# Expert blocks of at most 64 tokens with high and low parts side by side in one stationary operand

## The chip, the cores and the metric

The kernel runs on one core of a Trainium2 chip. The metric is the device time of one execution in microseconds. Before the change it is 1669.88 us, the median of three runs (1667.90 to 1670.72).

## What is computed

One layer over 1024 tokens of width 1024: a state-space branch and a short convolution, merged and projected, and then a mixture of 32 experts in four groups. Only the experts matter here. Each token goes to two experts of one group, and each expert computes on its tokens

```python
hid = jax.nn.silu(xblk @ w_gate[e]) * (xblk @ w_up[e])
return hid @ w_down[e]
```

with `w_gate` and `w_up` 1024 x 512 and `w_down` 512 x 1024, all in float32. The routing of the given inputs sends very different numbers of tokens to the experts. In the order in which the kernel works through them (`seq`) they are 194, 46, 56, 6, 140, 20, 55, 27, 77, 31, 47, 22, 106, 56, 48, 11, 143, 22, 8, 5, 117, 47, 32, 69, 62, 169, 106, 11, 193, 79, 12, 31. So 21 of the 32 have at most 64 tokens, 6 have 65 to 128, and 5 have more than 128; of these five second blocks three have at most 64 tokens (12, 15, 41), and two have 66 and 65.

## The kernel before, in words

The first half of the kernel (to about 885 us) computes the mixers and the routing. The rest is a Python loop over the 32 experts (from L1822, written out in full in the program). The order of the instructions on every engine is the order in which the code is written; no scheduler moves them.

Precision: a float32 operand is split into a high part `hi` (a ScalarE copy to fp32r, L91) and a low part `lo` (VectorE, source minus high part, L92). A product is then three matmuls (`mm3`, L94): high by high, high by low, low by high.

One expert's weights arrive as six tiles of 1 MB (`raw`, 128 x 2048), issued on SP's queue (`dma_w`, L1519) each time an older one has been split. `spl(e, i)` (L1655) splits tile `i` in two halves: two ScalarE copies of 128 x 1024 and two VectorE subtractions. That makes 12 ScalarE and 12 VectorE instructions for an expert.

A block of up to 128 tokens is gathered to `xg` (128 x 1024, one token a partition; partitions without a token keep zeros or old rows). `xhalf` (L1670) transposes half of it on TensorE into PSUM (`tp`) and splits it to `xh` and `xl`. `part(e, q, o)` (L1679) multiplies half `q` with the gate (`o` = 0) or up (`o` = 1) weights: four slices of three matmuls with 512 columns. The two halves add up in one PSUM bank for gate and one for up (`GU`). `act` (L1683) takes SiLU of the gate bank on ScalarE and multiplies it with the up bank on VectorE. `hsplit` (L1688) transposes the result on TensorE and splits it to `hh` and `hl`. `down` (L1696) is 24 matmuls into `ybank`; `emit` weights the rows and scatters them to DRAM from GpSimd.

The body of the loop interleaves expert e with expert e + 1: the second half of gate and up of e, then `spl(e + 1, 1)`, `act`, `spl(e, 4)`, the first half of gate of e + 1, `hsplit`, `spl(e, 5)`, the first half of up of e + 1, `down`, and three more splits. Three run-time conditions (`tc.If`) stand in it, for second blocks of experts with more than 128 tokens: L1831, L1844 and L1851 (which holds L1852 and L1858). Every engine executes the branch of every `If`, also one that has nothing in its body. The block count of an expert is read from SBUF into a register (`get_nb`, L1758).

Of the kernel before, what the change touches and what calls it, by code (L numbers as in the profile page):

```python
# [33 lines left out]
SLOTS = 128  # L34
NB = 8
# [14 lines left out]
def block_kernel(ctx: ExitStack, tc: tile.TileContext, I, out):  # L50
# [1201 lines left out]
    def pick(pl, i):  # L1252
        rr = sb(pl, "rr", [P, 2, 6, NE], BF16, bufs=3)
# [5 lines left out]
    def place(pl, i, b0, rr, ps):  # L1259
        oa = sb(pl, "oa", [P, 2, 2 * P], BF16, bufs=3)  # L1260
# [377 lines left out]
    by_seq = nbi.rearrange("p (g m) -> p m g", g=4)  # L1638
# [31 lines left out]
    def xhalf(xg, q, nm="x"):  # L1670
# [17 lines left out]

    def hsplit(hf, a="hh", b="hl"):
        a, b = sb(wk, a, [P, 4, P], F32R), sb(wk, b, [P, 4, P], F32R)  # L1690
# [27 lines left out]
    def over(e, q, banks):  # L1718
        if q == 0:
            warm(banks[0], 1.3)  # L1720
        xs = xhalf(xos[e % 2], q, "o")
        for o in range(2):
            part(e, q, o, xs, banks[o])

    full = xgs[0][:, 0:NB * NE * 3].rearrange("p (b e f) -> p b e f", b=NB, e=NE)

    def more(e, wf, banks, banks2):
# [21 lines left out]
        ht = tr(act(banks, "so"), "xf", 0)  # L1749
# [8 lines left out]
    def get_nb(e):  # L1758
        if e not in NBV:
            NBV[e] = load_nb(e)  # L1760
        return NBV[e]

    def load_pair(e):
        return nc.values_load(nbp[0:1, e:e + 1], min_val=0, max_val=NB)
# [3 lines left out]

    GU = [[sb(psm, f"{x}{i}", [P, FF]) for x in "gu"] for i in range(2)]
    ybank = [sb(psm, f"y{n}", [P, 512]) for n in range(2)]  # L1770
    warm(ybank[0], 4.7)
    XA = xhalf(xgs[0], 0)
    take_lo((2, 3), V)
    XB = xhalf(xgs[0], 1)
# [3 lines left out]
    for o in range(2):  # L1778
        part(0, 0, o, XA, GU[0][o])
    for x in xos:  # L1780
        G.memset(x, 0.0)
    take_lo((4, 5), V)
    for e in range(2):
        nb = get_nb(e)
        with tc.If(nb > 1):
# [6 lines left out]
    nb = get_nb(0)  # L1792
    with tc.If(nb > 1):
# [29 lines left out]
    for e in range(NE):  # L1823
# [3 lines left out]
        if nxt:  # L1827
            XA = xhalf(xgs[(e + 1) % NX], 0)
        part(e, 1, 1, XB, A[1])
        spl(e + 1, 1)  # L1830
        with tc.If(get_nb(e) > 1):  # L1831
            over(e, 1, B)
            sgo = act(B, "so")
# [3 lines left out]
        sg = act(A)  # L1837
        if nxt:
            spl(e, 4)
        if nxt:  # L1840
            part(e + 1, 0, 0, XA, B[0])
        hs = hsplit(sg)
        if e + 2 < NE:
            with tc.If(get_nb(e + 2) > 1):  # L1844
                gather(xos[e % 2], e + 2, 1)
        if nxt:
            spl(e, 5)
            XB = xhalf(xgs[(e + 1) % NX], 1)
            gather(xgs[(e + 1) % NX], e + 1 + NX, 0)
            part(e + 1, 0, 1, XA, B[1])  # L1850
        with tc.If((load_pair(e) if nxt else get_nb(e)) > 1):  # L1851
            with tc.If(get_nb(e) > 1):  # L1852
# [164 lines left out]
```

## Time and profile before

| | |
|---|---|
| median of three runs | 1669.88 us |
| the profiled execution | 1674.46 us, span 1672.6 us |
| TensorE matmul busy | 1570.5 us (94%) |
| VectorE busy | 1320.1 us (79%) |
| ScalarE busy | 725.3 us (43%) |
| GpSimd busy | 330.5 us (20%) |
| mean granted TensorE clock | 0.984 |
| DMA over the span | 381.61 MB, mean 228 GB/s |

The busy shares are means over stages that differ. The expert loop takes from about 885 us to 1610 us, so a change in it is read from a window inside it. An engine's row names the line of the code; the word after a window's busy times is the granted clock, then the share of the DMA engines' time.

### The profile page before, as it was taken

Reading aid. Unit: us, or ns where it says so; the run is one execution under the profiler, and the core shown is the slowest. Engines: PE = TensorE matmul, PEld = TensorE weight load, DVE = VectorE, ACT = ScalarE, POOL = GpSimd, SP = SyncE. Lnnn points to the kernel's source line nnn. Section 1 sums busy time; section 2 is a strip of 40 time slices with the busy share of each in tenths; the row PEclk is TensorE's granted clock in tenths of the full one; section 3 lists DMA queues with packets and bytes.
Section 4 is the critical chain, followed back from the end, with each engine's and each line's share of the span. In section 5 each row is a group of like instructions: output and inputs, shape, how many; then the busy total and the mean of one; then the engine's idle time right before and its main releaser. Section 6 shows DMA issues by size and latency. Waiting matters only on the chain.

```text
span 1672.6 us, 23420 instructions
## 1 busy us (share of the span) xinstructions
PE 1570.5 (94%) x7602; PEld 1237.4 (74%) x7602; DVE 1320.1 (79%) x2917; ACT 725.3 (43%) x1053; POOL 330.5 (20%) x264
## 2 busy tenths in 40 slices
PE   7899999899998899999988999999999999999984
PEld 3688888778886777788866777777777777777751
DVE  7858883569998568878876786999986999686877
ACT  1533332341213342231122664777764777465622
POOL 1431000002234300003213121221221212120127
PEclk9999999999998999999989999999999999999998
DMA  8425788742314665656524695999995999676872
GB/s 320 163 76 167 230 244 263 239 166 98 100 60 131 167 179 164 202 194 229 184 77 162 251 340 191 348 364 363 362 345 182 361 356 377 259 284 240 290 296 101
DMA packets 141731, 381.61 MB, mean 228 GB/s; under 512 B 17632, under 2 KB 76160, under 8 KB 116992
## 3 DMA queue, kind: packets, MB, share of 16 engines
q1 hardware_dynamic: 130912, 362.80, 62.2%
q0 software_dynamic: 10656, 16.80, 2.7%
q8 instruction: 83, 1.36, 0.3%
q14 instruction: 80, 0.66, 0.1%
HBM read 336.98 MB, written 68.76 MB: 243 GB/s over the span
## 4 chain that ended last, share of the span: by engine, by line
PE 34%; DMA 24%; issue 21%; DVE 17%; POOL 1%; SPq 1%; POOLq 1%; another core or an unknown queue 0%; ACT 0%; DVEq 0%; ACTq 0%
DMA y_d<-yt,tbi 13%; DMA xo<-h_d,tbi 8%; DVE vs L911 4%; DVE sa L908 4%; PE g L95 3%; PE g L97 3%; PE g L96 3%; PE t L97 2%; PE t L95 2%; PE t L96 2%; PE pm L95 1%; DVE vc L911 1%; PE pm L96 1%; PE pm L97 1%; DVE acc L784 1%
## 5 line engine op out<-in xcount | busy, mean ns | idle before, releaser
L92 DVE TENSOR_TENSOR lo<-raw,hi 128x1024 fp32r<-128x1024 f32 x376 | 440.9, 1221 | 31.5 <-ACT hi L91 21.4
L91 ACT ACTIVATE hi<-raw 128x1024 fp32r<-128x1024 f32 x376 | 372.0, 1051 | 34.0 <-PEq L1858 20.8
L95 PE MATMUL g<-hh,wh 128*128 128x512 f32 x448 | 177.1, 395 | 0.0
L96 PE MATMUL g<-hl,wh 128*128 128x512 f32 x448 | 174.7, 390 | 0.0
L97 PE MATMUL g<-hh,wl 128*128 128x512 f32 x448 | 174.6, 390 | 0.0
L1715 POOL DMA_INDIRECT y_d<-yt,tbi x37 | 92.3, 2495 | 382.0 <-DVE yt L1708 300.4
L95 PE MATMUL y<-hi,hh 128*128 128x512 f32 x256 | 103.0, 402 | 6.1 <-PEq L1858 2.1
L92 POOL TENSOR_TENSOR wl<-raw,wh 128x1024 fp32r<-128x1024 f32 x17 | 41.1, 2419 | 330.8 <-ACT wh L91 330.8
L95 PE MATMUL g<-hi,xh 128*128 128x512 f32 x256 | 102.5, 400 | 4.2 <-ACT xh L91 0.3
L95 PE MATMUL u<-hi,xh 128*128 128x512 f32 x256 | 105.8, 413 | 0.0
L97 PE MATMUL g<-hi,xl 128*128 128x512 f32 x256 | 100.6, 393 | 1.1 <-DVE xl L92 1.1
L97 PE MATMUL u<-hi,xl 128*128 128x512 f32 x256 | 100.9, 394 | 0.0
L97 PE MATMUL y<-hi,hl 128*128 128x512 f32 x256 | 100.5, 392 | 0.0
L96 PE MATMUL g<-lo,xh 128*128 128x512 f32 x256 | 100.3, 392 | 0.0
L96 PE MATMUL u<-lo,xh 128*128 128x512 f32 x256 | 99.9, 390 | 0.0
L96 PE MATMUL y<-lo,hh 128*128 128x512 f32 x256 | 99.8, 390 | 0.0
L91 ACT ACTIVATE xh<-tp 128x512 fp32r<-128x512 f32 x64 | 37.5, 588 | 140.7 <-PE tp L1675 140.7
L95 PEld LDWEIGHTS g<-hh,wh 128*128 128x128 f32 x448 | 84.3, 188 | 19.1 <-issue 2.3
L97 PEld LDWEIGHTS g<-hh,wl 128*128 128x128 f32 x448 | 84.2, 188 | 17.9
L96 PEld LDWEIGHTS g<-hl,wh 128*128 128x128 f32 x448 | 84.3, 188 | 16.7
L610 ACT ACTIVATE sg<-g 128x512 f32<-128x512 f32 x32 | 19.2, 599 | 140.1 <-PE g L97 104.8
L1551 POOL DMA_INDIRECT xg<-h_d,tbi x32 | 34.0, 1063 | 213.6 <-PE tp L1675 160.1
(503 smaller groups left out, 3581.6 us busy)
## 6 DMA issues: line engine op xcount, KB each, us to landing
raw<-in_w_exp SPq DMA_DIRECT2D x192, 1024.0 KB
raw<-in_w_r SPq DMA_DIRECT2D x28, 512.0 KB
w<-w_d SPq DMA_DIRECT2D x32, 384.0 KB
raw<-in_w_ada SPq DMA_DIRECT2D x20, 512.0 KB
sig_d<-sg SPq DMA_DIRECT2D x32, 256.0 KB
rp<-r_d SPq DMA_DIRECT2D x64, 128.0 KB
raw<-in_w_ada SPq DMA_DIRECT2D x6, 1024.0 KB
aw<-in_w_ada SPq DMA_DIRECT2D x12, 512.0 KB
```

What stands on the lines that cost most here:

```text
L91: S.activation(hi, src, AF.Copy)
L92: (eng or V).tensor_tensor(lo, src, hi.bitcast(F32), op=ALU.subtract)
L95: PE.matmul(ps, a[0], b[0], start=first, stop=False)
L96: PE.matmul(ps, a[0], b[1], start=False, stop=False)
L97: PE.matmul(ps, a[1], b[0], start=False, stop=last)
L610: S.activation(sg, pg, AF.Sigmoid)
L784: V.scalar_tensor_tensor(acc, w[:, k, :], sc[:, k, 0:1], acc, op0=ALU.mult, op1=ALU.add)
L908: V.tensor_tensor(t[d], cur[:, d].unsqueeze(2).to_broadcast([P, 2, 2, NPAIR]), kc[:, d], op=ALU.mult)
L911: V.tensor_tensor(new[:, d], new[:, d], t[d][:, r], op=ALU.add)
L1551: G.indirect_dma_start(out=xg, out_offset=None, in_=h2_d, in_offset=bass.IndirectOffsetOnAxis(ap=tbi[:, b, seq[e], 0:1], axis=0), bounds_c ...
L1715: G.indirect_dma_start(out=y_d, out_offset=bass.IndirectOffsetOnAxis(ap=tbi[:, b, seq[e], 1:2], axis=0), in_=yt, in_offset=None, bounds_ch ...
```

## The change

For a block of at most 64 tokens (`HB`), the high parts of the 64 token columns and their low parts stand side by side in one 128-column stationary operand `xh`. One matmul with the high weights and one with the low weights then give rows 0 to 63 (high part of the tokens) and rows 64 to 127 (low part), and the two halves of the rows are added later. The third matmul of each slice is left out for such blocks; for the others it follows in `part_low`. The addition happens in the step that transposes: `both` is two 64 x 64 identities on top of each other, and a matmul of 128 rows of the gate bank with it transposes and adds at once (`fold`). For that both banks are copied to SBUF first (`sg`, `us`), and SiLU and the product come behind the transposition, on 128 x 256. Which way a block goes is decided at run time: counts are now in units of 64 (`nbh`), and `xhalf`, `part_low`, `act` and `hsplit` each hold a `tc.If`.

```diff
+    nbh = iotab[:, 0:2 * NE].bitcast(I32)
+    V.tensor_scalar(nbh, pc, HB - 1.0, None, op0=ALU.add)
+    V.tensor_scalar(nbh, nbh, 6, None, op0=ALU.logical_shift_right)
...
+    both = sb(xgp, "both", [P, HB])
+    V.tensor_add(both, ident[:, 0:HB], ident[:, HB:P])
+
-    def xhalf(xg, q, nm="x"):
+    def xhalf(xg, q, nb, lim, nm="x"):
...
-        split(xh, xl, pt)
+        S.activation(xh, pt, AF.Copy)
+        with tc.If(nb < lim) as few:
+            V.tensor_tensor(xh[:, :, HB:P], pt[:, :, 0:HB], xh[:, :, 0:HB].bitcast(F32), op=ALU.subtract)
+        with few.Else():
+            V.tensor_tensor(xl, pt, xh.bitcast(F32), op=ALU.subtract)
         return xh, xl
 
     def part(e, q, o, xs, ps_):
         for z in range(4):
-            mm3(ps_, (xs[0][:, z, :], xs[1][:, z, :]), piece(e, 2 * q + o, z, FF), q == 0 and z == 0, q == 1 and z == 3)
-
-    def act(pgu, nm="sg"):
+            w = piece(e, 2 * q + o, z, FF)
+            PE.matmul(ps_, xs[0][:, z, :], w[0], start=(q == 0 and z == 0), stop=False)
+            if q == 0 or z < 3:
+                PE.matmul(ps_, xs[0][:, z, :], w[1], start=False, stop=False)
+
+    def part_low(e, q, xs, banks, nb, lim):
+        with tc.If(nb >= lim):
+            for o in range(2):
+                for z in range(4):
+                    PE.matmul(banks[o], xs[1][:, z, :], piece(e, 2 * q + o, z, FF)[0], start=False, stop=False)
+        if q:
+            for o in range(2):
+                PE.matmul(banks[o], xs[0][:, 3, :], piece(e, 2 + o, 3, FF)[1], start=False, stop=True)
...
+    def fold(sg, us, pt):
+        ps_ = flat(pt).rearrange("p (x k t) -> p x k t", x=2, k=4)
+        for x, src in enumerate((sg, us)):
+            for k in range(4):
+                PE.matmul(ps_[:, x, k], src[:, k * P:(k + 1) * P], both, start=True, stop=True)
+        S.activation(halves(sg), ps_[:, 0], AF.Silu)
+        V.tensor_mul(halves(sg), halves(sg), ps_[:, 1])
+
+    def act(banks, us, nb, lim, nm="sg", now=False):
         sg = sb(wk, nm, [P, FF])
-        S.activation(sg, pgu[0], AF.Silu)
-        V.tensor_mul(sg, sg, pgu[1])
+        with tc.If(nb < lim) as few:
+            S.activation(sg, banks[0], AF.Copy)
+            S.activation(us, banks[1], AF.Copy)
+            if now:
+                fold(sg, us, sb(psm, "tp", [P, 4, P], bufs=2))
+        with few.Else():
+            S.activation(sg, banks[0], AF.Silu)
+            V.tensor_mul(sg, sg, banks[1])
         return sg
...
+    def hsplit(sg, us, nb, lim, a, b):
         pt = sb(psm, "tp", [P, 4, P], bufs=2)
-        for k in range(4):
-            PE.transpose(pt[:, k, :], hf[:, k * P:(k + 1) * P], ident)
-        split(a, b, pt)
+        with tc.If(nb < lim) as few:
+            if us is not None:
+                fold(sg, us, pt)
+            split(a[:, :, 0:HB], b[:, :, 0:HB], halves(sg))
+        with few.Else():
+            for k in range(4):
+                PE.transpose(pt[:, k, :], sg[:, k * P:(k + 1) * P], ident)
+            split(a, b, pt)
         return a, b
...
         part(e, 1, 0, XB, A[0])
         if nxt:
-            XA = xhalf(xgs[(e + 1) % NX], 0)
+            XA = xhalf(xgs[(e + 1) % NX], 0, get_nb(e + 1), 2)
         part(e, 1, 1, XB, A[1])
+        part_low(e, 1, XB, A, get_nb(e), 2)
+        us = sb(wk, "us", [P, FF])
         spl(e + 1, 1)
-        with tc.If(get_nb(e) > 1):
+        with tc.If(get_nb(e) > 2):
...
-        sg = act(A)
+        sg = act(A, us, get_nb(e), 2)
...
-        hs = hsplit(sg)
+        hs = hsplit(sg, us, get_nb(e), 2, *HS)
...
             part(e + 1, 0, 1, XA, B[1])
+            part_low(e + 1, 0, XA, B, get_nb(e + 1), 2)
```

How this moves the instructions is seen in the built programs. First ScalarE, in the body of one expert from the second block's `If` to the next pair of weight splits; `sg` is SiLU's result, `hi` the high part of a weight half, `hh` that of the hidden rows, `tp` the PSUM tile of a transposition. Before:

```order
L1831 COMPARE_AND_BRANCH
L91 ACTIVATE oh_11728<-tp 128x512
L1685 ACTIVATE so<-g_9272 128x512
L1831 UNCONDITIONAL_BRANCH x2
L1685 ACTIVATE sg<-g_9274 128x512
L91 ACTIVATE hi<-raw 128x1024 x2
L91 ACTIVATE hh<-tp 128x512
L1767 TENSOR_LOAD nbi
L1844 COMPARE_AND_BRANCH
L1844 UNCONDITIONAL_BRANCH x2
L91 ACTIVATE hi<-raw 128x1024 x2
```

The same stretch with the change, from behind the second block's `If` (the rows between a COMPARE_AND_BRANCH and the first UNCONDITIONAL_BRANCH are the way of at most 64 tokens, those up to the second one the other way):

```order
L1723 ACT_TABLE_LOAD
L1723 ACTIVATE sg<-g_9280 128x512
L1724 ACTIVATE us<-u_9281 128x512
L1722 UNCONDITIONAL_BRANCH
L1728 ACT_TABLE_LOAD
L1728 ACTIVATE sg<-g_9280 128x512
L1722 UNCONDITIONAL_BRANCH
L92 ACT_TABLE_LOAD
L92 ACTIVATE hi<-raw 128x1024 x2
L1738 COMPARE_AND_BRANCH
L1717 ACT_TABLE_LOAD
L1717 ACTIVATE sg<-tp 128x256
```

and, a few rows later, behind the condition on the gather of a second block (L1902) and ahead of the splits of tile 5:

```order
L1825 TENSOR_LOAD iotab
L1902 COMPARE_AND_BRANCH
L1902 UNCONDITIONAL_BRANCH x2
L92 ACT_TABLE_LOAD
L92 ACTIVATE hi<-raw 128x1024 x2
```

Between the same weight splits stand activation-table loads that were not there: four on the way of at most 64 tokens (L1723, L92, L1717, L92) and three on the other (L1728, L92, L92), in every expert of the loop. In the whole program there are 7 such rows before and 295 now.

Second TensorE, from the first half of gate of expert e + 1 to the first half of its up product, before:

```order
L97 MATMUL g_9272<-hi,xl_9777 128x512
L1693 MATMUL tp<-ident,sg 128x128 x4
L1767 TENSOR_LOAD nbi
L1844 COMPARE_AND_BRANCH
L1844 UNCONDITIONAL_BRANCH x2
L1675 MATMUL tp<-ident,xg_9271 128x128 x4
L95 MATMUL u_9273<-hi,xh_9776 128x512
```

and with the change:

```order
L1695 MATMUL g_9280<-lo,xh_9833 128x512
L1738 COMPARE_AND_BRANCH
L1716 MATMUL tp<-both,sg 128x64 x4
L1716 MATMUL tp<-both,us 128x64 x4
L1738 UNCONDITIONAL_BRANCH
L1744 MATMUL tp<-ident,sg 128x128 x4
L1738 UNCONDITIONAL_BRANCH
L1825 TENSOR_LOAD iotab
L1902 COMPARE_AND_BRANCH
L1902 UNCONDITIONAL_BRANCH x2
L1682 MATMUL tp<-ident,xg_9273 128x128 x4
L1684 COMPARE_AND_BRANCH
```

The four transpositions stand in one arm of a condition, eight folding matmuls in the other, and a further condition follows the transpositions of the next block; in an expert's body each engine passes six conditions more than before (L1684 twice, L1698 twice, L1722, L1738).

## Rows read from the trace of the kernel before

**Rows 1.** The page: busy time, share of the span and count of each engine.

```profile
PE 1570.5 (94%) x7602; PEld 1237.4 (74%) x7602; DVE 1320.1 (79%) x2917; ACT 725.3 (43%) x1053; POOL 330.5 (20%) x264
```

**Rows 2.** Windows, two experts without a second block; the first line names the columns.

```profile
core 0: us, PE busy (x) PEld busy (x) DVE busy (x) ACT busy (x) POOL busy (x), PEclk, DMA share, GB/s
1100.10:1118.74 18.64, 18.34 (x86) 14.59 (x85) 17.70 (x19) 13.86 (x16) 3.89 (x3) 1.00 0.99 370
1156.03:1174.66 18.63, 18.33 (x86) 14.57 (x85) 17.71 (x19) 13.86 (x16) 3.89 (x3) 1.00 0.98 361
```

**Rows 3.** Waits, 1081.45 to 1193.30 us (six experts): us in total, times, longest.

```profile
ACT xh L91 <- PE tp L1675: 19.5, 6, 3.3
ACT hh L91 <- PE tp L1693: 7.5, 6, 1.3
PEld y L95 <- ACTq L1851: 3.3, 6, 0.6
```

**Rows 4.** Groups of instructions, the same six experts, ScalarE and VectorE.

```profile
L91 ACT ACTIVATE hi<-raw 128x1024 fp32r<-128x1024 f32 x72 | 70.9, 1050 | 0.9 <-ACTq L1851 0.7
L91 ACT ACTIVATE hh<-tp 128x512 fp32r<-128x512 f32 x6 | 3.6, 599 | 7.5 <-PE tp L1693 7.5
L92 DVE TENSOR_TENSOR xl<-tp,xh 128x512 fp32r<-128x512 f32 x12 | 8.2, 684 | 0.0
```

**Rows 5.** Timeline, TensorE in the same expert: start us, us, instruction.

```profile
1103.63 0.40 PE L97 MATMUL u<-hi,xl 128*128 128x512 f32 x1
1104.18 0.47 PE L95 MATMUL g<-hi,xh 128*128 128x512 f32 x1
...
1107.02 0.60 PE L1693 MATMUL tp<-ident,sg 128*128 128x128 f32 x4
1107.46 0.60 PE L1675 MATMUL tp<-ident,xg 128*128 128x128 f32 x4
...
1111.75 0.39 PE L95 MATMUL y<-hi,hh 128*128 128x512 f32 x1
...
1116.33 0.39 PE L97 MATMUL y<-hi,hl 128*128 128x512 f32 x1
```

**Rows 6.** Timeline, ScalarE in the first expert (in its second block, and behind it).

```profile
918.13 1.28 ACT L1685 ACT_TABLE_LOAD   x1
921.51 0.60 ACT L1685 ACTIVATE so<-g 128x512 f32<-128x512 f32 x1 [2.09 <-PE g L97]
922.12 1.28 ACT L1685 ACT_TABLE_LOAD   x1
923.42 0.60 ACT L1685 ACTIVATE sg<-g 128x512 f32<-128x512 f32 x1
```

**Rows 7.** Groups by form: the nearest instructions of 128 x 256 that read PSUM.

```profile
L882 ACT ACTIVATE vj<-t 128x256 f32<-128x256 f32 x32 | 12.3, 385 | 6.1 <-PE t L97 5.0
L92 DVE TENSOR_TENSOR ul<-t,uh 128x256 fp32r<-128x256 f32 x16 | 6.7, 422 | 10.1 <-ACT uh L91 10.1
```

**Rows 8.** Timeline, ScalarE in an expert without a second block.

```profile
1101.79 2.00 ACT L91 ACTIVATE hi<-raw 128x1024 fp32r<-128x1024 f32 x2
1103.91 0.60 ACT L1685 ACTIVATE sg<-g 128x512 f32<-128x512 f32 x1
1104.40 2.00 ACT L91 ACTIVATE hi<-raw 128x1024 fp32r<-128x1024 f32 x2
```

**Rows 9.** Windows, the first expert's second block (columns as in rows 2).

```profile
899.70:902.20 2.50, 0.00 (x0) 0.01 (x1) 0.70 (x1) 0.00 (x0) 1.59 (x1) 1.00 0.87 323
904.30:907.40 3.10, 3.10 (x8) 2.44 (x8) 2.36 (x2) 1.07 (x2) 0.00 (x0) 0.50 0.91 374
```

**Rows 10.** One tensor's instructions (the index table `tbi`): gathers of second blocks.

```profile
L1551 POOL DMA_INDIRECT xo<-h_d,tbi x5: 999/1750/1777, 892.8 to 1486.6; - x5
```

**Rows 11.** Timeline, VectorE ahead of the expert loop.

```profile
887.62 0.18 DVE L1635 TENSOR_SCALAR nbi<-misc 128x32 int32<-128x32 f32 x1
887.84 1.74 DVE L1636 TENSOR_SCALAR nbi<-nbi 128x32 int32<-128x32 int32 x1
```

More of the change, by code (lines that the diff above doesn't have):

```diff
@@ L34 @@
 SLOTS = 128
+HB = 64
 NB = 8
@@ new lines, in flat, with halves @@
+    def flat(t_):
+        return t_.rearrange("p a b -> p (a b)")
+    def halves(sg):
+        return sg[:, 0:4 * HB].rearrange("p (k t) -> p k t", k=4)
+    def fold(sg, us, pt):
[5 more added lines that the diff above has]
+        V.tensor_mul(halves(sg), halves(sg), ps_[:, 1])
@@ new lines, in act @@
+    def act(banks, us, nb, lim, nm="sg", now=False):
+        sg = sb(wk, nm, [P, FF])
+        with tc.If(nb < lim) as few:
[6 more added lines that the diff above has]
+            V.tensor_mul(sg, sg, banks[1])
+        return sg
+    HS = [sb(wk, x, [P, 4, P], F32R) for x in ("hh", "hl")]
@@ L1691, in hsplit @@
+    for t_ in HS:
+        G.memset(t_.bitcast(F32), 0.0)
+    def hsplit(sg, us, nb, lim, a, b):
         pt = sb(psm, "tp", [P, 4, P], bufs=2)
-        for k in range(4):
-            PE.transpose(pt[:, k, :], hf[:, k * P:(k + 1) * P], ident)
-        split(a, b, pt)
+        with tc.If(nb < lim) as few:
[6 more added lines that the diff above has]
+            split(a, b, pt)
@@ L1748, in more @@
                               start=(q == 0 and z == 0), stop=(q == 1 and z == 3))
-        ht = tr(act(banks, "so"), "xf", 0)
+        so = sb(wk, "so", [P, FF])
+        S.activation(so, banks[0], AF.Silu)
+        V.tensor_mul(so, so, banks[1])
+        ht = tr(so, "xf", 0)
         for k in range(4):
@@ L1779, in block_kernel @@
         part(0, 0, o, XA, GU[0][o])
+    part_low(0, 0, XA, GU[0], get_nb(0), 2)
     for x in xos:
@@ L1791, in block_kernel @@
     scatter(zt, NE - 1, 0)
-    nb = get_nb(0)
-    with tc.If(nb > 1):
+    with tc.If(get_nb(0) > 2):
         over(0, 0, GU[1])
@@ L1827, in block_kernel @@
         if nxt:
-            XA = xhalf(xgs[(e + 1) % NX], 0)
+            XA = xhalf(xgs[(e + 1) % NX], 0, get_nb(e + 1), 2)
         part(e, 1, 1, XB, A[1])
+        part_low(e, 1, XB, A, get_nb(e), 2)
+        us = sb(wk, "us", [P, FF])
         spl(e + 1, 1)
-        with tc.If(get_nb(e) > 1):
+        with tc.If(get_nb(e) > 2):
             over(e, 1, B)
-            sgo = act(B, "so")
+            sgo = act(B, us, get_nb(e), 4, "so", True)
         if not nxt:
@@ L1847, in block_kernel @@
             spl(e, 5)
-            XB = xhalf(xgs[(e + 1) % NX], 1)
+            XB = xhalf(xgs[(e + 1) % NX], 1, get_nb(e + 1), 2)
             gather(xgs[(e + 1) % NX], e + 1 + NX, 0)
             part(e + 1, 0, 1, XA, B[1])
-        with tc.If((load_pair(e) if nxt else get_nb(e)) > 1):
-            with tc.If(get_nb(e) > 1):
-                h_ = hsplit(sgo, "oh0", "ol0")
+            part_low(e + 1, 0, XA, B, get_nb(e + 1), 2)
+        with tc.If((load_pair(e) if nxt else get_nb(e)) > 2):
+            with tc.If(get_nb(e) > 2):
+                h_ = [sb(wk, x, [P, 4, P], F32R) for x in ("oh0", "ol0")]
+                for t_ in h_:
+                    G.memset(t_.bitcast(F32), 0.0)
+                hsplit(sgo, None, get_nb(e), 4, *h_)
                 banks = [sb(psm, "tp", [P, 512], bufs=2) for _ in range(2)]
@@ L1857, in block_kernel @@
             if nxt:
-                with tc.If(get_nb(e + 1) > 1):
+                with tc.If(get_nb(e + 1) > 2):
                     over(e + 1, 0, A)
```

26 lines of the change are left out of this document (12 added, 14 removed).

## Prediction

> **What bounds the kernel now.** The page's busy shares come first [rows 1]: TensorE 94%, ScalarE only 43%. They are means over the whole kernel, so the reader should go to windows of the expert loop. An expert without a second block takes 18.64 us, again and again [rows 2], and there TensorE is busy for 18.34 of it, VectorE for 17.70, ScalarE for 13.86, at a granted clock of 1.00 (the upper level, 2.4 GHz), and the DMA engines for 0.98 to 0.99 of their time. The waits say which of the four ends last: ScalarE waits for TensorE's transpositions (19.5 + 7.5 us in six experts), TensorE for no engine's data, only at branches (0.55 us at L1851) [rows 3]. So TensorE sets the pace. VectorE is 0.9 us behind it, the DMA engines 0.2 to 0.4 us, and ScalarE has 18.64 - 13.86 = 4.78 us of room in an expert. These three rooms are what the change has to live with.
>
> A matmul's record lasts 0.39 us, but 20 of them start within 1116.33 - 1111.75 = 4.58 us [rows 5]: one costs 0.229 us. The 72 of an expert are 16.5 us; the rest of the 18.64 is transpositions and gaps at branches.
>
> **What it takes away.** For a block of at most 64 tokens, 16 of the 48 gate and up matmuls go: 16 x 0.229 = 3.7 us of TensorE. VectorE works on half the columns four times (two `xl`, the product, `hl`): 0.68 becomes 0.42 [rows 4, 7], about 1.0 us. It applies to 21 of 32 experts (token counts above).
>
> **What it adds on ScalarE** decides. On the way of at most 64 tokens, each term in us an expert:
> - four activation-table loads at 1.28 [rows 6]: +5.13. They are nearly pure time: the load at 922.12 ends at 923.40, the next instruction starts at 923.42. The table that it loaded was the one that the condition's arm had loaded 4 us earlier for the same function, so a load that changes nothing cost the same;
> - two copies of a bank in place of one SiLU, at 0.60 each [rows 8]: +0.60;
> - SiLU over 128 x 256, 0.385 [rows 7]: +0.39;
> - `hh` over 256 columns, 0.60 to the same 0.39 [rows 4, 7]: -0.21.
>
> 13.86 + 5.91 = 19.77 us of ScalarE work, over 18.64 before anything waits. To it come a lost overlap (ScalarE instructions overlap by 0.1: the one at 1103.91 lasts 0.60, the next starts at 1104.40 [rows 8]; table loads don't), 0.1; the wait of `hh` for VectorE's product, which now stands between SiLU and `hh` with nothing in between: 0.42 [rows 7] and some 0.1 for the two handovers, 0.5; and six more conditions. The two splits at 1101.79 end at 1103.79 and SiLU starts at 1103.91 [rows 8], so L1831 cost ScalarE 0.12 us; I take 0.1 for each, 0.6 (bounds 0 and 1.9, by TensorE's 0.32 a condition below). Together 21.0 us: **ScalarE becomes the bound**, 2.36 us over the old period.
>
> TensorE in such an expert needs about 18.64 - 3.7 + 0.5 + 1.0 = 16.4 us: four transpositions and a condition take 0.44 us [rows 5], eight folding matmuls on half the columns in their place at most about 0.9, and the conditions some 1.0. It is idle some 4 us in 21. After 2.5 us of idleness at 899.70 its granted clock was 0.50 (the lower level, 1.2 GHz) from 904.30 to 907.40 [rows 9], 8 matmuls in 3.1 us, where 1.83 would do at the upper level. The longest idle stretch lies between the second half of `up` and the first half of gate of the next expert, which waits for VectorE's `xh`; at half the clock those eight matmuls take 1.3 us longer, and ScalarE's third load waits for the fold behind them. Nothing in ScalarE's order hides more than about 1 us there. Bounds 0 and 1.1; I take 0.4.
>
> So 2.8 us for an expert. The last of the 21 has no next expert beside it, and its 3.7 us from TensorE stand against two loads, copy and fold in a row: nothing. 20 x 2.8 = **56 us**.
>
> **The 6 experts of 65 to 128 tokens** keep all 72 matmuls. ScalarE gets three loads: 13.86 + 3.85 + 0.6 = 18.3, still below TensorE. TensorE has the six conditions; from 1103.63 to 1104.18 the step is 0.55 instead of 0.229 [rows 5], so L1831 cost 0.32 us there. Some are empty on TensorE and lie between matmuls already queued: 0.2 each, 1.2 us. And the transpositions of `sg` come sooner after the last gate and up matmul: eight matmuls stand between, 1.83 us, not twelve, while SiLU has a load ahead of it: 1.28 + 0.60 + 0.68 + 0.3 = 2.9 us; less 1.83 and a branch leaves 0.8. Together 2.0 us (bounds 0.8 and 3.5): 6 x 2.0 = **12 us**.
>
> **The 5 experts with a second block** (five gathers `xo` [rows 10]): 2.0 as above, six more conditions in the second block at 0.2, 1.2; in three of them 3.7 us of matmuls go, against 1.2 for two copies that TensorE now waits for and 0.9 for the fold, mean -0.9 over the five. With 0.1 for a load on their longer chains, 2.4 (bounds 0.5 and 5): **12 us**.
>
> **Start and tail.** Ahead of the loop VectorE gets two more integer operations on 32 columns, like the rows of 0.18 and 1.74 us [rows 11], and the first transposition's split now waits for the count: 2 us (bounds 0.5 and 4). The rest of the program is the same; the smaller pools of `pick` and `place` act in code that these counts do not reach.
>
> **Sum.** 56 + 12 + 12 + 2 = 82 us. The profiled execution took 1674.46 us (span 1672.6), so it would take 1756.5; the median shown is 4.6 us below the profiled one, and 1669.88 + 82 gives 1752. With the low ends: 20 x 1.13 (19.77 - 18.64, no wait at all) + 6 x 0.8 + 5 x 0.5 + 0.5 = 30, 1700. With the high ends: an expert at 2.36 + 0.6 (conditions at 0.2) + 1.1 = 4.1 x 20 = 81, + 21 + 25 + 4 = 131, 1801.
>
> **Rivals.**
> A, not slower: the loads cost ScalarE next to nothing (the set is active already, or they run while ScalarE waits in any case), so that its sum is 19.77 - 5.13 = 14.6 and the old bounds hold. In a small expert TensorE falls to 16.4 and VectorE to 17.7 - 1.0 + its 0.9 of waits + 0.5 of branches = 18.1; the DMA engines stay at 0.98 x 18.64 = 18.3 and decide: -0.35 x 20 = -7. With conditions as cheap on TensorE as L1831 is on ScalarE, 0.1, the larger six cost 6 x 0.6 = 3.6 and the second blocks 5 x (1.2 - 0.9) = 1.5: 1669.88 - 2 = 1668. It decides from the point where the four loads together add less than 1 us to an expert. For it: ScalarE has 4.78 us of room, and it waits 4.5 us for transpositions in each expert [rows 3]. Against it: rows 6 show 1.28 us twice, and the loads and the copies together want 5.9 us.
>
> B, a change of the set costs more than the load. In rows 6 nothing stands between the load's end and the next instruction but 0.02 us; however, ScalarE had waited before one of the loads. If a change of the set had to empty the engine at as much again as the load itself, two of the four loads of a small expert change it: 2 x 1.28 x 20 = 51 us more, and 1.28 more on the chain of the 11 others, 14: 1752 + 65 = 1817. The Trainium skill has such a rule (ScalarE: Activation LUTs, What ACT_TABLE_LOAD costs): a load of about 1283 ns and a drain of about 1380 ns, 2.66 us for every switch. The trace agrees with the 1283 and shows no drain behind either of the loads of rows 6; by that rule the sum would be 2.76 us a small expert more, an estimate from that page of some 1822.
>
> C, TensorE's clock. If it falls twice in an expert (both idle stretches) and the second fall reaches `down`, which ScalarE then waits for through the next transpositions, an expert costs 2.36 + 2 x 1.3 [rows 9] = 5.0 and the sum is 20 x 5.0 + 26 = 126: 1796, and up to 1830 where one more stretch of an expert falls. For it: 4 us of idleness in 21. Against: `down` waits for VectorE's low halves anyway.
>
> **How the numbers follow.** The forecast with its bounds, 1700 to 1801, has 0.80: its lower end needs only the loads' measured 1.28 us and the in-order ScalarE. A has 0.06, B 0.06, C 0.08. The range 1700 to 1802 leaves out B, A, half of C and a twentieth of the forecast, 0.2 together. Under 0.2% (3.3 us) a measurement of this kernel can't tell from no change. Slower by more: forecast, B and C, 0.94, less 0.01 for a forecast that misses all its waits: 0.93. A's 0.06 lies on both sides of that limit: faster 0.03, the same 0.03 and the 0.01.
>
> **What would show it.** In the new profile: ScalarE rows ACT_TABLE_LOAD by the hundred (about 21 x 4 + 11 x 3 = 117 and a few in the second blocks), 1.28 us each, 150 us busy; the period of two neighbouring small experts at 21 us with ScalarE busy over 19 and TensorE under 17.5; DMA share below 0.9 there; VectorE waiting for `hi`. If the period is 18.3 with DMA at 1.00, A holds; if gaps stand behind the loads, B; if the granted clock in small experts is below 0.9 and ScalarE waits for TensorE's fold or transpositions, C. The forecast is wrong if the small experts' period is at or below 18.64, or if the 11 others move more than the 21.

## The result, and the profile after

The changed kernel takes 1809.03 us (median of four runs, 1807.16 to 1814.91) against 1669.39 before, in four runs each: ratio 1.0843, interval 1.0814 to 1.0871. That is 139.6 us slower. The forecast was 82 us slower, 1752, in a range up to 1802: the side was right, and so was the cause, table loads on ScalarE; what they cost was not, in small experts and above all in experts with a second block.

The page of the profiled execution (1814.91 us, span 1813.1), the row that answers to [rows 1] and the granted clock in 40 slices:

```profile
PE 1585.1 (87%) x7506; PEld 1230.4 (68%) x7506; DVE 1293.6 (71%) x2920; ACT 894.5 (49%) x1220; POOL 345.3 (19%) x276
PEclk9999999999999999999888899999999999899987
```

ScalarE has 169 us more to do than before, TensorE has lost 96 matmul records and yet shows 15 us more, and from the 20th slice on the clock is below 0.9 of full speed in seven slices (before in two). What ScalarE has in addition stands in the groups of the loop (columns as in rows 4, with up to three releasers):

```profile
L92 ACT ACT_TABLE_LOAD x63 | 80.8, 1283 | 6.7 <-issue 5.8 <-ACTq L1890 0.2
L1717 ACT ACT_TABLE_LOAD x24 | 30.8, 1283 | 31.0 <-issue 20.1 <-PE tp L1716 10.8
L1723 ACT ACT_TABLE_LOAD x20 | 25.7, 1283 | 5.2 <-ACTq L1890 2.4 <-DVE lo L93 2.0 <-PEq L1890 0.7
L1728 ACT ACT_TABLE_LOAD x13 | 16.7, 1283 | 20.1 <-PE g L1704 18.7 <-DVE lo L93 1.3
```

120 table loads at 1.283 us are 154.0 us of the 169. The windows that answer to [rows 2] (columns there), three small experts, a large one (65 to 128 tokens) and one with a second block:

```profile
1216.47:1238.44 21.97, 18.74 (x92) 14.82 (x92) 17.26 (x19) 19.96 (x23) 3.89 (x3) 1.00 0.82 299
1106.32:1128.56 22.24, 18.60 (x81) 13.63 (x80) 16.72 (x19) 19.69 (x23) 3.91 (x3) 0.92 0.81 297
1398.39:1421.52 23.13, 19.35 (x81) 15.51 (x80) 16.72 (x19) 19.74 (x23) 3.88 (x2) 0.85 0.78 284
1443.49:1462.22 18.73, 15.20 (x70) 11.62 (x69) 17.16 (x19) 16.22 (x19) 4.38 (x2) 1.00 0.91 334
1332.66:1374.64 41.98, 33.10 (x139) 25.80 (x137) 19.88 (x24) 21.50 (x25) 5.52 (x6) 0.88 0.41 143
```

In these three small experts ScalarE is the fullest engine, at 19.7 to 20.0 us, as the forecast's 19.77 had it; the DMA engines have fallen to 0.8. But the period is 22 to 23, not 21: ScalarE waits for more than was counted. Its timeline in the third of these windows:

```profile
1399.23 1.28 ACT L1723 ACT_TABLE_LOAD   x1 [0.24 <-ACTq L1890]
1400.52 0.60 ACT L1723 ACTIVATE sg<-g 128x512 f32<-128x512 f32 x1
1401.01 0.59 ACT L1724 ACTIVATE us<-u 128x512 f32<-128x512 f32 x1
1401.62 1.28 ACT L92 ACT_TABLE_LOAD   x1
1402.92 2.00 ACT L92 ACTIVATE hi<-raw 128x1024 fp32r<-128x1024 f32 x2
1407.10 1.28 ACT L1717 ACT_TABLE_LOAD   x1 [2.17 <-issue]
1408.39 0.38 ACT L1717 ACTIVATE sg<-tp 128x256 f32<-128x256 f32 x1
1409.26 0.42 ACT L92 ACTIVATE hh<-sg 128x256 fp32r<-128x256 f32 x1 [0.49 <-DVE sg L1718]
1409.98 1.28 ACT L92 ACT_TABLE_LOAD   x1 [0.30 <-issue]
```

and TensorE's at the same time:

```profile
1400.86 0.47 PE L1693 MATMUL g<-hi,xh 128*128 128x512 f32 x1 [2.43 <-DVE xh L1685]
...
1402.92 0.63 PE L1695 MATMUL g<-lo,xh 128*128 128x512 f32 x1
1403.38 1.94 PE L1716 MATMUL tp<-both,sg 128*128 128x64 f32 x8
1405.11 1.91 PE L1716 MATMUL tp<-both,us 128*128 128x64 f32 x8
```

TensorE stands 2.43 us for VectorE's lower halves; from 1402.09 on its matmuls start some 0.43 us apart, where the first six were 0.23 apart; and the fold (four instructions in each row; they appear as eight records) takes 3.4 us to the next instruction's start; ScalarE's third load comes 2.17 us late. In the first of the windows above the clock stays at 1.00, and the whole is about a microsecond shorter.

The periods by kind of expert, each from one output scatter to the next, mean in us. The first expert is counted from the first gather `xg` of the start to its output scatter, so that it holds the start of the loop.

| | 16 small | 4 small, the next has a second block | 6 large | 4 with a second block | the first (second block, and the start) |
|---|---|---|---|---|---|
| before | 18.78 | 26.41 | 18.88 | 33.35 | 60.82 |
| after | 22.70 | 31.58 | 19.92 | 40.36 | 76.75 |
| difference, all of them | 62.7 | 20.7 | 6.2 | 28.0 | 15.9 |

These make 133.5 of the 140.5 us between the two spans. 3.6 lie ahead of the first gather, which came at 885.06 before and at 888.66 after, and at 878.9 to 887.3 in the other profiles of this study, so that this part differs from one execution to the next; some 3 lie behind the scatter of the last expert but one.

### The profile page after: what moved, and what is told of

It reads as the page before. It is cut to its first block, busy times and chain, and to the rows that moved or that the text cites. A ratio compares the mean times of both kernels' runs of the same rounds, so it can differ in the third digit from the quotient of the medians.

```text
span 1813.1 us, 25483 instructions
## 1 busy us (share of the span) xinstructions
PE 1585.1 (87%) x7506; PEld 1230.4 (68%) x7506; DVE 1293.6 (71%) x2920; ACT 894.5 (49%) x1220; POOL 345.3 (19%) x276
## 5 line engine op out<-in xcount | busy, mean ns | idle before, releaser
L92 ACT ACTIVATE hi<-raw 128x1024 fp32r<-128x1024 f32 x376 | 371.2, 1048 | 53.6 <-PEq L1920 30.4
L1693 PE MATMUL g<-hi,xh 128*128 128x512 f32 x256 | 112.4, 439 | 54.1 <-DVE xh L1685 20.7
L1693 PEld LDWEIGHTS g<-hi,xh 128*128 128x128 f32 x256 | 52.8, 206 | 76.3 <-issue 39.2
L1695 PE MATMUL u<-lo,xh 128*128 128x512 f32 x224 | 90.4, 403 | 0.2 <-DVE lo L93 0.2
L1552 POOL DMA_INDIRECT xg<-h_d,tbi x32 | 44.2, 1382 | 239.7 <-PE tp L1682 213.1
L92 ACT ACT_TABLE_LOAD x63 | 80.8, 1283 | 6.7 <-issue 5.8
L96 PEld LDWEIGHTS y<-hi,hh 128*128 128x128 f32 x256 | 49.1, 192 | 51.6 <-ACT hh L92 20.8
```

Of the source, the lines that this page charges most:

```text
L92: S.activation(hi, src, AF.Copy)
L96: PE.matmul(ps, a[0], b[0], start=first, stop=False)
L1552: G.indirect_dma_start(out=xg, out_offset=None, in_=h2_d, in_offset=bass.IndirectOffsetOnAxis(ap=tbi[:, b, seq[e], 0:1], axis=0), bounds_c ...
L1693: PE.matmul(ps_, xs[0][:, z, :], w[0], start=(q == 0 and z == 0), stop=False)
L1695: PE.matmul(ps_, xs[0][:, z, :], w[1], start=False, stop=False)
```

## The experiments

The theory after the result: the table loads make nearly all of it, by filling ScalarE in small experts and by standing in the chain of the experts with second blocks. Rivals: the six conditions with the waits at their ends; TensorE's clock. All ratios are to the kernel before, run on the same chip. Line numbers in the rows of an experiment are those of its own code.

**No loads: e1_one_silu.** At the end of a condition whose arms leave different tables, the built program loads the table anew in whatever comes next. If SiLU's table is there before the loop, every arm leaves it.

```diff
     warm(ybank[0], 4.7)
+    pre = sb(wk, "pre", [P, 1])
+    S.activation(pre, ident[:, 0:1], AF.Silu)
     XA = xhalf(xgs[0], 0, get_nb(0), 2)
```

> The changed kernel with one tiny SiLU (128 x 1) ahead of the expert loop, outside every condition. The table that holds SiLU also holds the copy, so both arms of every condition then leave the same table behind, and the program has no table load inside the loop: 120 executed loads become 1. Conditions, folds, waits and matmuls stay. Theory (the loads are the cause, by filling ScalarE in small experts and by standing in the chain of experts with a second block): small experts come down from 22.7 us to about 18.5, between 18.3 (the DMA engines at 0.98 of the old 18.64) and 18.9; those with a second block from 48.4 to about 39; total 1678, between 1655 and 1700. Rival 1 (the six conditions and the waits that stand at their ends): loads were only in places where ScalarE waited anyway, total above 1750. Rival 2 (TensorE stands idle for VectorE's lower halves, its clock falls, and ScalarE waits for a fold at half the clock): small experts stay above 21 us with granted clocks of 0.85 to 0.92, total above 1740.

Measured: 1700.44 us, 1.0180 (1.0161 to 1.0199). This one instruction gives back 109 of the 139.6 us. The mean periods are 19.28, 27.01, 18.23 and 35.81, the first expert 69.84 (order as in the table). The total is 0.4 us above the theory's range, and small experts stay above the 18.9 that it allowed them; but the loads are the bulk, as it said, and both rivals fall as causes of the bulk. Two windows, one small and one large expert:

```profile
1145.90:1165.07 19.17, 16.83 (x83) 13.01 (x82) 16.62 (x19) 14.85 (x19) 3.92 (x2) 1.00 0.94 345
1184.50:1202.39 17.89, 16.12 (x74) 12.61 (x73) 17.07 (x19) 13.89 (x16) 4.04 (x2) 1.00 0.98 376
```

In the small one no engine is full. The engines wait for each other, as ScalarE's timeline there shows:

```profile
1152.94 0.38 ACT L1717 ACTIVATE sg<-tp 128x256 f32<-128x256 f32 x1 [2.06 <-PE tp L1716]
1154.10 0.42 ACT L92 ACTIVATE hh<-sg 128x256 fp32r<-128x256 f32 x1 [0.78 <-DVE sg L1718]
```

and TensorE's fold ahead of that SiLU, up to the next instruction:

```profile
1150.89 1.07 PE L1716 MATMUL tp<-both,sg 128*128 128x64 f32 x8 [0.44 <-ACT hi L92]
...
1152.69 0.61 PE L1682 MATMUL tp<-ident,xg 128*128 128x128 f32 x4
```

TensorE waits for VectorE's lower half, ScalarE for the fold behind it, VectorE for ScalarE's high parts behind that, and the next lower half comes behind these: a ring, as read from the waits. The later runs test it only in part.

**The clock: e2_warm_gap.**

```diff
...
+        if keep:
+            with many.Else():
+                last()
+                warm(ybank[0], 2.2)
...
```

> The changed kernel, with five matmuls on the identity (some 2.2 us by the program's own count) put behind the last gate and up matmuls of every main block of at most 64 tokens, in the gap in which TensorE waits for VectorE's lower halves. They write a bank that nothing reads; the two closing matmuls move into the arms of the condition that is there already, so no condition is added. Theory (loads): TensorE's granted clock in small experts rises from 0.85-0.92 to 1.00, the fold takes 1.75 us for its eight matmuls in every one, and ScalarE's wait ahead of the SiLU falls by up to 1.5 us where the clock had halved; with ScalarE at 19.7 us busy a small expert cannot go below some 21.5: 22.7 becomes 21.8, total 1790, between 1780 and 1812. Rival 2 (TensorE's clock is the cause): small experts go to 20 or less, total below 1765. Rival 1 (conditions): within 5 us of the changed kernel's 1809.

Measured: 1810.02 us, 1.0829 (1.0803 to 1.0854), small experts 22.60. The clock did what was wanted, 1.00 in all sixteen small windows, as in this one:

```profile
1207.22:1229.19 21.97, 20.47 (x100) 16.06 (x99) 17.25 (x19) 19.95 (x23) 4.41 (x3) 1.00 0.86 301
```

but ScalarE's first load now waited for the added matmuls, here in the expert ahead of it:

```profile
1187.08 1.28 ACT L1732 ACT_TABLE_LOAD   x1 [0.93 <-PE y L102]
```

So the run has a cost of its own, and bounds the clock's part only roughly. The total lies in the theory's range and also within the 5 us that rival 1 (conditions) allowed: it speaks against the clock alone. In the changed kernel itself ten of the 16 small windows have granted clocks of 0.85 to 0.93 and a mean of 22.92 us, six have 1.00 and 22.34: some 0.6 us in ten experts, 6 us. The experts with a second block and those ahead of them have 0.84 to 0.96 there, and 1.00 before; the clock's part in these was not separated. The clock isn't the cause of the 140.

**The loads alone: e3_loads_in_before.** In the kernel before:

```diff
+    def swap(i, fn):
+        S.activation(tiny[i], ident[:, 0:1], fn)
...
+        if nm == "sg":
+            swap(0, AF.Exp)
         S.activation(sg, pgu[0], AF.Silu)
...
+        if nm == "hh":
+            swap(1, AF.Exp)
         split(a, b, pt)
+        if nm == "hh":
+            swap(2, AF.Silu)
```

> The kernel before, with four table loads in every expert and nothing else of the change: a tiny exponential (128 x 1) ahead of SiLU and one ahead of hh, each of which makes the next SiLU load its table again (a tiny SiLU stands behind hh). No condition, no fold, all 72 matmuls. ScalarE's sum is 13.86 + 4 x 1.28 + 4 tiny ones, some 19.5 to 19.8, as much as in a small expert of the changed kernel. Theory (loads): an expert goes from 18.64 to 20.5, between 19.8 and 21.3; total 1669 + 31 x 1.9 = 1728, between 1705 and 1755; what the changed kernel's small experts have beyond that (22.7) is fold, clock and joins. Rival 1 (conditions): loads fit in ScalarE's 4.78 us of waits, total below 1685. Rival 2 (clock): below 1700, granted clock 1.00.

Measured: 1758.35 us, 1.0514 (1.0482 to 1.0546), a little above the theory's range. Small experts 21.07, large 21.45, with a second block 38.20:

```profile
1188.94:1209.53 20.59, 19.41 (x87) 14.74 (x86) 17.79 (x19) 19.76 (x25) 4.47 (x3) 1.00 0.86 321
1301.60:1339.90 38.30, 33.16 (x143) 26.17 (x141) 21.34 (x24) 21.18 (x26) 4.39 (x3) 0.91 0.43 150
```

Where the forecast's way of counting applies (the sum passes the period) it is nearly right: 19.76 of work, 20.6 us in this window. In the second row ScalarE is busy for 21.2 of 38.3 us, and four loads (5.1 us, with the tiny activations some 5.9) still cost 4.9 us: there most of their length lies in the chain.

**Loads and conditions, without the small way: e4_all_large.**

```diff
     V.tensor_scalar(nbh, nbh, 6, None, op0=ALU.logical_shift_right)
+    V.tensor_scalar(nbh, nbh, 2, None, op0=ALU.max)
```

> The changed kernel with the count of half blocks raised to at least two, so that every main block takes the way of more than 64 tokens: all 48 gate and up matmuls, transpositions instead of folds, but every condition of the change and three loads an expert. Second blocks are as in the changed kernel. Theory (loads): three loads and no copies are 17.7 us of ScalarE, below TensorE's 18.34, so a former small expert costs what the large ones of the changed kernel cost, 18.9 to 19.9; with 9.5 us for each second block and 3 for the start total 1725, between 1705 and 1750. Rival 1 (conditions and joins): they are all still run, so total 1790 or more. Rival 2 (clock): no gap at the low halves, clock 1.00, total within 10 us of the theory's, so this run does not tell those two apart.

Measured: 1764.71 us, 1.0557 (1.0532 to 1.0581): above the theory's range and below the rival's, a miss for both. Two neighbours:

```profile
1156.57:1177.34 20.77, 19.88 (x91) 15.44 (x90) 17.69 (x19) 19.02 (x22) 4.83 (x2) 1.00 0.94 334
1177.34:1196.96 19.62, 17.21 (x79) 13.27 (x78) 17.70 (x19) 16.17 (x18) 4.45 (x3) 1.00 0.97 357
```

The mean is 20.6, so that in a row of large experts three loads and six conditions cost 1.8 us each, although ScalarE's sum, 17.6 in the mean of these two and 18.0 over all 22 windows, is below the old period. I had expected less from the large experts of the changed kernel, of which three take 18.7; that is what a large expert takes between small ones.

**Conditions without loads: e5_conditions_alone.** The edits of e1 and e4 together.

> No table load in the loop (one tiny SiLU ahead of it) and the count of half blocks raised to at least two: every main block takes the way of more than 64 tokens, so it has the six conditions and nothing else of the change (second blocks as in the changed kernel). Prediction of record: six conditions at 0.2 us on TensorE, so a former small expert would cost 18.64 + 1.2 = 19.8, total near 1669 + 31 + 17 = 1717. Theory after the first four runs (TensorE no longer waits ahead of conditions that are empty on it; large experts took 17.9 to 18.9 without loads): conditions cost 0.1 each at most, a main block 18.6 to 19.1, second blocks 2.6 more each as in e1, total 1669 + 13 + 3 + 5 = 1690, between 1680 and 1700. Rival (the conditions are all that is left of the 30 us): total 1700 or more, small experts 19.3 as in e1.

Measured: 1698.67 us, 1.0157 (1.0138 to 1.0176), at the upper edge of the theory's range. Former small experts take 19.17, large ones 19.16, with a second block 34.81:

```profile
1145.70:1164.93 19.23, 18.43 (x86) 14.59 (x85) 17.87 (x19) 13.87 (x16) 2.76 (x3) 1.00 0.97 351
```

Six conditions cost 0.3 to 0.4 us of a main block, not 1.2. And the small way's 19.28 in e1 is no less than the large way's 19.17 here, under the same conditions and without loads: in a small expert **the 16 saved matmuls buy nothing**, and the rival's last clause is right that far. Something is gained beside it and lost again: the large experts take 18.23 among small ones (e1) and 19.16 here, those with a second block 35.81 in e1 and 34.81 here. The whole kernel is no faster with the saved matmuls (1.0180, here 1.0157).

**Second blocks as before: e6_second_old.** `over` and what follows it get the matmuls, SiLU and transpositions of the kernel before, with no condition inside.

```diff
...
-            sgo = act(B, us, get_nb(e), 4, "so", True)
+            sgo = sb(wk, "so", [P, FF])
+            S.activation(sgo, B[0], AF.Silu)
+            V.tensor_mul(sgo, sgo, B[1])
...
```

> One tiny SiLU ahead of the loop, and second blocks as in the kernel before: no condition inside them, all their matmuls, SiLU and transpositions as before. Main blocks as in the changed kernel. Theory (the second block's folds, copies and conditions stand in a chain that nothing hides): the five experts with a second block come from 41.5 to 39.5 and the four ahead of them from 27.0 to 26.6; total 1700 - 11 = 1689, between 1683 and 1695. Rival (it is the main block's conditions there, or its neighbour's small way): within 4 us of 1700. Second rival (the matmuls saved in the three second blocks of at most 64 tokens are worth more than what they add): slower than e1, above 1704.

Measured: 1692.67 us, 1.0114 (1.0095 to 1.0132). Experts with a second block come from 35.81 to 33.02, below the 33.35 of before; the four ahead of them don't gain (27.56). The second block is better off without its small way.

**The ring: e7_hi_ahead_of_fold and e8_e6_and_e7.**

`spl_hi` makes the two high parts of a weight tile alone; `spl` then adds the low parts.

```diff
...
             spl(e, 4)
+            spl_hi(e, 5)
             part(e + 1, 0, 0, XA, B[0])
```

> One tiny SiLU ahead of the loop, and two of the next high parts (the first `down` weights' second pair, spl(e, 5)) copied on ScalarE ahead of the fold's SiLU instead of behind hh; VectorE's order stays. In e1 ScalarE stands 2.06 us for the fold and 0.78 for the product in a small expert, and then VectorE stands 0.94 for the high parts that queue behind. Theory (without the loads a small expert is paced by this ring: low half, matmuls, fold, SiLU, product, hh, high parts, low parts, next low half): VectorE's 0.94 goes, and some of its 0.89; small experts go from 19.28 to 18.3, large ones stay at or below 18.9; total 1700 - 18 = 1682, between 1674 and 1692. Rival (small experts are paced by the conditions, or by the DMA engines at 0.94): no change, 1696 to 1704.

> Both: the second blocks as before and the two high parts ahead of the fold, with the one tiny SiLU ahead of the loop. Theory: the two gains lie in different experts and add, 1700 - 11 - 18 = 1671, between 1660 and 1680, about the kernel before. Rival (they take from the same wait): no better than the better of the two by more than 4 us.

Measured: e7 1699.71 us, 1.0159 (1.0129 to 1.0189), no change in the total; e8 1687.37 us, 1.0090 (1.0072 to 1.0107), above its range and 5 us below e6. In e7 small experts gained 0.4 us (18.89), less than half of what the ring theory gave, and large ones lost 0.9 (19.14), since their `hh` now stands behind the two copies. VectorE's wait for the high parts is one link of the ring and not the one that decides.

**Where a load costs: f2_two_loads_at_copies and f3_two_loads_at_fold.** Two loads go back into e1, in small experts alone, once ahead of the copies and once ahead of the fold's SiLU. ScalarE's sum is the same in both.

```diff
+    def two_loads():
+        S.activation(tiny[0], ident[:, 0:1], AF.Exp)
+        S.activation(tiny[1], ident[:, 0:1], AF.Silu)
...
+                two_loads()
             S.activation(sg, banks[0], AF.Copy)
```

> e1 (no table load in the loop), with two table loads put back in small experts alone: a tiny exponential and a tiny SiLU ahead of the two copies of the banks. ScalarE's sum in a small expert becomes some 14.6 + 2 x 1.28 + 2 x 0.2 = 17.6 us, still 1.7 below the 19.28 that a small expert takes in e1. Theory of the prediction of record (ScalarE costs time only where its sum passes the other engines): nothing, 19.3 us, total 1700, within 5. Theory of the ring (ScalarE's instructions from the copies to the next high parts lie in the chain that paces a small expert; loads add to it wherever ScalarE isn't waiting): e1 has room of some 1.9 us between the end of the copies and the fold that reads them, but the high parts queue behind the copies, so that 1 to 2.4 of the 2.96 us land; small experts 20.3 to 21.7, total 1700 + 20 x 1.7 = 1734, between 1720 and 1750.

> The same two loads, the same sum of ScalarE, in another place: ahead of the fold's SiLU, where ScalarE stood 2.06 us for the fold in e1. Theory of the prediction of record (the sum decides): 1700, within 5, the same as the other place. Theory of the ring: the wait takes 2.06 of the 2.96 us, 0.9 lands; small experts 20.2, total 1718, between 1710 and 1728, and below the other place by some 15.

Measured: f2 1734.46 us, 1.0366 (1.0339 to 1.0393), small experts 21.00; f3 1731.25 us, 1.0333 (1.0293 to 1.0373), small experts 20.81. So 2.96 us of ScalarE cost 1.5 to 1.7 us in an expert that kept it some 15 of 19.3 us busy: **the sum does not decide**. The ring's forecast was right for f2 and wrong for f3, where the fold should have hidden more. ScalarE in an expert of f3:

```profile
1107.94 1.28 ACT L1709 ACT_TABLE_LOAD   x1
1109.24 0.20 ACT L1709 ACTIVATE tiny<-ident 128x1 f32<-128x1 f32 x1
1109.45 1.28 ACT L1710 ACT_TABLE_LOAD   x1
1110.74 0.20 ACT L1710 ACTIVATE tiny<-ident 128x1 f32<-128x1 f32 x1
1110.85 0.37 ACT L1723 ACTIVATE sg<-tp 128x256 f32<-128x256 f32 x1
```

The fold ended about 1109.0 there, so SiLU came 1.9 us after it: the wait that I had counted as 2.06 us of room was 1.0 us in this expert. (Over the twenty small experts of e1 it was 1.7 in the mean, 1.1 to 2.6.)

**Toward a version that keeps up: f4_three_conditions and f5_gathers_first.** f4 takes e6, puts the closing products, the second block, and SiLU or the copies under one condition, the second lower half and the low products under another, and e7's two high parts into the small arm alone.

```diff
...
+        with tc.If(get_nb(e) < 2) as few:
+            last(e, XB, A)
+            S.activation(sg, A[0], AF.Copy)
+            S.activation(us, A[1], AF.Copy)
+        with few.Else():
+            low(e, 1, XB, A)
+            last(e, XB, A)
+            with tc.If(get_nb(e) > 2):
+                over(e, 1, B)
...
```

> A version that might reach the kernel before: no table load in the loop, second blocks as before, three conditions of the change in an expert in place of six (closing products, second block and SiLU or copies under one; VectorE's low half of the second x transposition and the low products under one; the fold's), and the two high parts of e7 ahead of the fold in the small arm alone, behind hh in the large one. Theory (conditions cost 0.4 to 0.5 us an expert in e5, and e7's order cost large experts 0.9): small experts 18.4, the floor of the DMA engines at 0.98 to 0.99; large ones 18.0; second blocks as in e8; start +3. Total 1673 - 7 - 5 + 5 = 1666 beside a kernel before at 1673, ratio 0.990 to 1.003. Rival (the number of conditions doesn't matter, what is left are the waits that the small way itself adds): as e8, ratio 1.007 or more.

Measured: 1680.07 us, 1.0049 (1.0031 to 1.0067), between theory and rival. Large experts come to 18.22, small ones stay at 18.83.

f5 is f4 with GpSimd's order at the start restored. In the changed kernel GpSimd, which has no work in the first conditions, waits at the first of them for the counts, and two more zeroings stand ahead of the gather of the second block. GpSimd's timeline after:

```profile
888.66 1.26 POOL L1552 DMA_INDIRECT xg<-h_d,tbi  x1 [25.75 <-DVE sgm L1285]
...
894.18 0.95 POOL L1834 MEMSET xg<- 128x1024 f32 x1 [3.25 <-DVE nbp L1645]
...
901.75 3.12 POOL L1552 DMA_INDIRECT xo<-h_d,tbi  x1 [0.16 <-remote]
```

and who waits for it, on TensorE:

```profile
912.56 1.09 PE L1682 MATMUL tp<-ident,xo 128*128 128x128 f32 x4 [7.25 <-DMA xo<-h_d,tbi]
```

```diff
+    for e in range(1, NX):
+        G.memset(xgs[e], 0.0)
+        gather(xgs[e], e, 0)
+    for x in xos:
+        G.memset(x, 0.0)
     XA = xhalf(xgs[0], 0, get_nb(0), 2)
```

> f4 with GpSimd's queue ahead of the loop put back in the order of the kernel before: the gathers of the next two experts and the zeroing of the second blocks' tiles ahead of the first two conditions, the zeroing of the two new operand halves behind the gather of the second block. In the changed kernel that gather starts 13.1 us after the first gather of the start, before it started 7.8 after it, since GpSimd waits at the first condition for the counts (3.25 us) and zeroes two more tiles. Theory (the start costs 5 us, not the 2 of the prediction): the gather starts 8 to 9 us after the first, TensorE's wait for it falls from 7.2 to some 3 us, and the kernel gets 4 us faster than f4: ratio 1.0025, between 1.000 and 1.004. Rival (TensorE's work at the start has room elsewhere): as f4, 1.005.

Measured: 1671.86 us, 1.0000 (0.9987 to 1.0013), as fast as the kernel before and 137 us faster than the change as it was. The gather starts 7.78 us after the first one, TensorE no longer waits for it, and the first expert takes 62.54 in place of f4's 67.17. That is 4.6 of the 5.5 us between the two profiled executions; the medians differ by 8.2, of which the rest was not located. Two of its windows, a small and a large expert:

```profile
1136.57:1154.93 18.36, 15.89 (x81) 12.68 (x80) 16.72 (x19) 14.23 (x18) 3.89 (x2) 1.00 1.00 380
1099.41:1117.39 17.98, 16.35 (x77) 12.94 (x75) 17.17 (x19) 13.77 (x16) 4.05 (x2) 1.00 1.00 378
```

Here TensorE has 1.6 to 2.5 us to spare, and the DMA engines have none: this is about the floor that rival A had named (18.3), and a likely reason why the saved matmuls can't be turned into time. It is not shown for the mean: f5's other small windows have DMA shares of 0.92 to 1.00, and no run takes bytes away.

## Why the forecast was right and wrong

- **What bounds the kernel.** Right, and more so than I used it: the period of 18.64 us, TensorE's 18.34 in it, stood only some 0.3 above the DMA engines' busy time (0.98 to 0.99 of it). With the loads gone and three of the conditions, f5's small experts take 18.82 on average against 18.78 before, 18.36 at a DMA share of 1.00.
- **The loads** on ScalarE: 120 against 117 and a few, at 1.28 us. Right. Taking them out gives 109 us back. Rival B is out: loads between an exponential and a SiLU, which have to change the table (f3's rows above, at 1107.94 and 1109.45), and loads of SiLU's table behind a SiLU (L1728 at 1347.89, below) all last 1283 ns, and no more than 0.03 us stands ahead of them or behind them. The rows that the forecast had used could not show this: behind the first load of [rows 6], the one that could have changed the table, ScalarE stood 2.09 us for TensorE. The Trainium skill (ScalarE: Activation LUTs, What ACT_TABLE_LOAD costs) adds a drain of about 1380 ns to a change of the set; no run here shows one. The Trainium skill (ScalarE: Activation LUTs, Table sets: the hidden batching unit) says that copies are in every set, and e1 agrees: with SiLU's table in place, no copy of the loop loads another.
- **Small experts**, 20 x 2.8 = 56: measured 83.4, 4.2 each. ScalarE's sum was right (19.77; 19.7 to 20.0 in the windows above, 20.3 in the mean of the sixteen, some of which hold work of a neighbour). Two steps failed. "Nothing in ScalarE's order hides more than about 1 us there" left the wait for the fold at 0.4: it is 1.0 in the mean of the twenty (none in seven, 0.8 to 3.3 in the others). The fold, estimated at "at most about 0.9" us from the time of transpositions, takes 1.8 at the upper clock (1150.89 to 1152.69 in e1) and 3.4 at the lower. And the period was built as ScalarE's sum plus its waits, as if the rest of the kernel would otherwise keep 18.64; in fact the small way has a ring of its own, 19.28 us without a load (e1), and loads come on top of that ring (f2, f3: half to 0.6 of their length; four loads in the changed kernel: 3.4 of 5.1 us).
- **Rival C** was right about the fall of the clock after TensorE's 2.43 us of idleness, and that ScalarE then waits for the fold; at some 6 us in the small experts it is a small part.
- **Large experts**, 6 x 2.0 = 12: measured 6.2. In a row of such experts the term comes out (e4: 1.8), but by luck: two errors cancel. Three loads cost 1.4 there (e4 less e5), not the 0.8 of one wait, and six conditions 0.3 to 0.4, not 1.2. Beside small experts, as in the changed kernel, it is 1.0.
- **Second blocks**, 5 x 2.4 = 12, bounds 0.5 and 5: measured 28.0 in four experts, 7.0 each, and 10.6 in the first (its 15.9 less the 5.3 of the start). This is the largest miss for an expert and the one farthest beyond its bounds. The step that failed was "0.1 for a load on their longer chains". ScalarE there, in the changed kernel:

```profile
1346.19 1.28 ACT L1717 ACT_TABLE_LOAD   x1 [1.64 <-PE tp L1716]
1347.48 0.38 ACT L1717 ACTIVATE so<-tp 128x256 f32<-128x256 f32 x1
1347.89 1.28 ACT L1728 ACT_TABLE_LOAD   x1
...
1349.80 1.28 ACT L92 ACT_TABLE_LOAD   x1
...
1353.60 1.28 ACT L92 ACT_TABLE_LOAD   x1
...
1357.28 0.40 ACT L92 ACTIVATE oh<-so 128x256 fp32r<-128x256 f32 x1
```

  VectorE, which follows ScalarE's high parts with its splits and comes to the next expert's lower half behind them:

```profile
1355.98 2.36 DVE L93 TENSOR_TENSOR lo<-raw,hi 128x1024 fp32r<-128x1024 f32 x2 [0.84 <-ACT hi L92]
1358.26 0.42 DVE L1685 TENSOR_TENSOR xh<-tp,xh 128x256 fp32r<-128x256 f32 x1
```

  and TensorE, which has too few matmuls of the next expert to cover it, between `so` and the second block's `down`:

```profile
1347.92 0.79 PE L1693 MATMUL g<-hi,xh 128*128 128x512 f32 x1 [1.81 <-ACT so L1717]
...
1358.83 0.77 PE L96 MATMUL tp<-hi,oh 128*128 128x512 f32 x1 [4.72 <-DVE xh L1685]
```

  ScalarE works without a gap of note from 1346.19 to 1357.68, four loads among it; VectorE's last split and the lower half come behind, and TensorE idles 4.72 us up to that. By the runs, loads are 4.6 of the 7.0 (e1), and the second block's own small way 2.8 (e6); the two make a little more than the whole.
- **Conditions.** 0.2 each was too much: 0.3 to 0.4 us for six (e5).
- **The start**, 2 us, bounds 0.5 and 4: 5.3 by the delay of the gather, 4.6 by f4 and f5. I had followed VectorE's and TensorE's queues to the first condition, not GpSimd's.
- **The sum.** 56 + 12 + 12 + 2 became 83.4 + 6.2 + 38.6 + 5.3 = 133.5; some 6 of the 139.6 lie outside these terms. Against the high ends (81, 21, 25 and 4) the second blocks are 13.6 over, at 2 to 5.6 us each, small experts 2.4, the start 1.3, and the large experts 14.8 under: without the miss in the second blocks the total, 7 us above the range, would have lain in it. The high end also took the conditions at 0.2 each and not at their own bound of 1.9 in all; with that it would have been 1815, but the conditions were not what cost.

Left open: why small experts ahead of a second block stay 0.8 us slower in f5 than before (27.16 against 26.41), and which link of the ring in e1 decides.

## What to carry to other kernels

A run-time condition whose arms leave different activation tables made this program load a table behind it, every time; look for the loads in the built program's order, and give all arms one table before the loop, where one holds all their functions. Busy sums tell which engine can't be passed, not what an instruction costs: ask of each added one whether its engine has a wait just there that it can use. And before work is taken from the fullest engine, ask how far below it the next stands: here 0.3 us, against an estimated 3.7 taken away.

## What the runs showed of the hardware

- A table load costs 1283 ns whether it has to change the table (exponential and SiLU, f3) or loads SiLU's again (1347.89 in the changed kernel), and the instruction behind it starts 0.02 us later.
- The fold's float32 matmul with 64 columns takes about 0.225 us at the upper clock (eight in 1.8 us in e1), as long as one of 512 columns with fp32r operands (0.229).
- An engine waits at a condition for its count also where it has no work in either arm (GpSimd, 3.25 us).
